# Attention's query projection as seven Strassen products, its sums placed beside the keys' product

## The chip, the cores and the metric

The kernel runs on one core of one Trainium2 chip, in one launch. The metric is the device time of one execution in microseconds (us). The core has five engines with queues of their own: TensorE (PE) for matmuls, VectorE (DVE), ScalarE (ACT), GpSimd (POOL), and SyncE (SP), from whose queue the large transfers are issued. Matmuls read SBUF and write PSUM, and only DVE and ACT take results out of PSUM in this kernel.

## The reference, cut to what matters

One encoder layer is applied to two groups of 256 tokens, so the kernel has 512 rows of 1024 channels. After a layer norm, one wide projection `x @ w_in` gives the inputs of three branches (an mLSTM, a grouped-query attention, a cross-attention into 256 memory tokens). The branches are projected, gated, added and projected once more. A residual layer norm and a gated convolutional feed-forward network follow. The change is in one slice of `x @ w_in`, the attention's queries:

```python
proj = x @ w_in
q_m, k_m, v_m, o_m, g_m, q_a, k_a, v_a, q_c, g_br = split_cols(proj, IN_SPLITS)   # q_a: 1024 columns
qa = apply_axial_rope(rms_norm(q_a.reshape(B, T, ATTN_HEADS, ATTN_DH), attn_q_norm_g), ang_r, ang_c)
ka = apply_axial_rope(rms_norm(k_a.reshape(B, T, KV_HEADS, ATTN_DH), attn_k_norm_g), ang_r, ang_c)
h_a = blocked_attention(qa.reshape(B, T, KV_HEADS, ATTN_GROUP, ATTN_DH), ka, v_a.reshape(B, T, KV_HEADS, ATTN_DH))
```

## The kernel before

**Matmuls.** Every large product is done in three terms. Both operands are split into a high part, rounded to the matmul's type by a cast on ACT, and a low part, the difference, by a subtraction on DVE. The three terms are high x high, high x low and low x high. A weight chunk is 128 x 1024 values: `load_chunk` (L97) loads it into a ring of three tiles "raw", and `split_chunk` (L110, L111) splits it into rings "hi" and "lo" of six tiles each. The transposed input xT has eight k tiles of 128 channels, each a pair of high and low tiles of 128 x 512.

**Jobs.** The program is a list of jobs. `add_nat` makes one for each pair of k tiles (24 matmuls of 512 columns). Its results, one PSUM bank for each of four row tiles, are evacuated in the last job. `run_jobs` (L188) runs the jobs in order and, after each of them, takes steps from the queue `side`, so many that it is empty at the next flush: here one step for each job. In this stretch the jobs are four of the cross-attention's queries ("qc"), one that queues the cross-attention's steps, four of the keys and values ("kv"), four and four of the attention's queries ("qa", "qb"), one that queues the attention's steps, and then the gates and branches ("gc", "bc" and so on).

**Side steps.** The cross-attention has eight units, four heads by two groups, in eleven steps (`attend`). Step i does the values of unit i-2, the transposes of unit i-1 ("pt", L422) and the scores of unit i ("sc"). Scores are followed by maximum (L401), exponentials (L405), reciprocal (L409) and scaling (L411). The transposed probabilities are split into "probTh" and "probTl" (L84, L85). `ev_rope` copies a result out of PSUM into a tile "rx" (L767) and queues a step that normalises and rotates it (L779 to L800). The keys' four such steps stand in `side` behind the cross-attention.

**What sets the order.** Outside a block at the start that is ordered by hand, the tile framework lays down each engine's order before the run. It goes by the order of the program, but lets later instructions pass one whose operands or tile are not there yet. Tiles of one tag share one ring and are handed out in the order in which the program asks for them. Rings that matter here: "a" (62 tiles of 128 x 512: activations, probabilities, "rx"), "hi", "lo" and "raw" for weights, and two in PSUM of four banks each, "pd" for large products and "pa" for scores, transposes and values. On the chip each engine then runs its list strictly in order.

The feed-forward network's down projection (L1120 and on) is already done in Strassen's form over seven pairs of its k tiles, with a transfer that adds in flight on POOL's queue (L1187).

## Time and profile before

| | us |
|---|---|
| median of 3 runs | 943.24 |
| lowest and highest run | 941.63, 943.36 |
| the profiled execution | 943.72 |
| its span (first to last instruction) | 941.9 |
| PE busy | 927.8 |
| DVE busy | 601.2 |
| ACT busy | 408.2 |
| POOL busy | 105.1 |

The span lies 1.8 us below the time of the profiled execution, which is 0.5 us above the median. A matmul of 512 columns is drawn 0.39 us long while the next one starts earlier, so the cost of a matmul has to be read from one start to the next. Weight loads run beside the matmuls.

### The profile page before, as it was taken

Reading aid. Unit: us, or ns where it says so; the run is one execution under the profiler, and the core shown is the slowest. Engines: PE = TensorE matmul, PEld = TensorE weight load, DVE = VectorE, ACT = ScalarE, POOL = GpSimd, SP = SyncE. Lnnn points to the kernel's source line nnn. Section 1 sums busy time; section 2 is a strip of 40 time slices with the busy share of each in tenths; the row PEclk is TensorE's granted clock in tenths of the full one; section 3 lists DMA queues with packets and bytes.
Section 4 is the critical chain, followed back from the end, with each engine's and each line's share of the span. In section 5 each row is a group of like instructions: output and inputs, shape, how many; then the busy total and the mean of one; then the engine's idle time right before and its main releaser. Section 6 shows DMA issues by size and latency. Waiting matters only on the chain. (4 is left out here: it accounts for less than half of the span.)

```text
span 941.9 us, 12380 instructions
## 1 busy us (share of the span) xinstructions
PE 927.8 (99%) x4633; PEld 788.8 (84%) x4633; DVE 601.2 (64%) x1139; ACT 408.2 (43%) x765; POOL 105.1 (11%) x106
## 2 busy tenths in 40 slices
PE   8999999999999999999999999999999999999995
PEld 6888888888889998888888889988888888888885
DVE  4584444896777535366667649655565655666998
ACT  4562543434555435344335312533333333445860
POOL 0100100350000000122007401000000000013301
PEclk9999999999999999999999999999999999999998
DMA  8354223224211243433235432333333333386522
GB/s 291 90 157 144 79 68 90 70 66 120 65 46 44 66 134 90 122 104 111 68 102 189 132 114 68 111 103 99 90 101 100 90 102 100 127 263 133 101 58 89
DMA packets 126671, 101.27 MB, mean 108 GB/s; under 512 B 4240, under 2 KB 106644, under 8 KB 126612
## 3 DMA queue, kind: packets, MB, share of 16 engines
q1 hardware_dynamic: 123588, 94.99, 33.3%
q0 software_dynamic: 3024, 5.51, 3.5%
q8 instruction: 36, 0.59, 0.3%
q14 instruction: 23, 0.19, 0.1%
HBM read 92.86 MB, written 2.11 MB: 101 GB/s over the span
## 5 line engine op out<-in xcount | busy, mean ns | idle before, releaser
L111 DVE TENSOR_TENSOR wlo<-raw,whi 128x1024 fp32r<-128x1024 f32 (+3 forms) x148 | 176.1, 1194 | 213.5 <-ACT whi L110 213.3
L110 ACT CAST whi<-raw 128x1024 fp32r<-128x1024 f32 (+3 forms) x148 | 148.2, 1009 | 298.7 <-PE ua L123 72.0
L1187 POOL DMA_DIRECT2D b<-b x21 | 18.6, 947 | 291.0 <-ACT xop L1227 272.5
L1281 PE MATMUL dn<-wop,xop 128*128 128x512 f32 (+1 forms) x105 | 39.5, 376 | 1.0 <-DVE y L1272 1.0
L1282 PE MATMUL dn<-wop,xop 128*128 128x512 f32 (+1 forms) x105 | 39.4, 375 | 0.0
L1283 PE MATMUL dn<-wop,xop 128*128 128x512 f32 (+1 forms) x105 | 39.3, 375 | 0.0
L1228 DVE TENSOR_TENSOR wop<-b,wop 128x512 fp32r<-128x512 f32 x49 | 33.0, 684 | 6.6 <-ACT wop L1227 6.5
L405 ACT ACTIVATE prob<-sc,nmax 128x256 f32<-128x256 f32 x48 | 22.5, 476 | 24.8 <-DVE nmax L401 24.8
L1227 ACT CAST wop<-b 128x512 fp32r<-128x512 f32 x49 | 29.5, 617 | 7.2 <-PE dn L1283 2.8
L1108 ACT ACTIVATE up<-up 128x512 f32<-128x512 f32 x22 | 13.9, 633 | 42.4 <-DVE up L476 42.4
L115 POOL TENSOR_TENSOR rss<-rss,mhalf 128x4 f32<-128x4 f32 (+1 forms) x12 | 22.6, 1886 | 75.5 <-DVE rss L784 75.5
L1281 PEld LDWEIGHTS dn<-wop,xop 128*128 128x128 f32 x105 | 19.8, 188 | 4.9 <-DVE y L1272 1.3
L1282 PEld LDWEIGHTS dn<-wop,xop 128*128 128x128 f32 x105 | 19.8, 188 | 3.6
L1283 PEld LDWEIGHTS dn<-wop,xop 128*128 128x128 f32 x105 | 19.8, 188 | 3.6
L401 DVE TENSOR_REDUCE nmax<-sc 128x2 f32<-128x512 f32 x24 | 16.4, 682 | 4.3 <-PE sc L124 4.3
L1186 ACT ACTIVATE b<-b 128x512 f32<-128x512 f32 x21 | 13.0, 630 | 11.8 <-DVE b L1190 8.5
L115 POOL TENSOR_TENSOR lnmv<-lnmv,mhalf 128x1 f32<-128x1 f32 x8 | 7.5, 942 | 90.6 <-DVE lnmv L297 90.6
L85 DVE TENSOR_TENSOR probTl<-pt,probTh 128x512 fp32r<-128x512 f32 x24 | 16.4, 683 | 1.4 <-ACT probTh L84 1.4
L473 DVE SCALAR_TENSOR_TENSOR up<-ub,col,up 128x510 f32<-128x510 f32 x20 | 14.9, 743 | 2.7 <-ACT up L470 2.7
L996 DVE SCALAR_TENSOR_TENSOR gate<-gate,ba 128x512 f32<-128x512 f32 x8 | 5.5, 686 | 17.1 <-PE ba L124 9.2
L334 POOL TENSOR_TENSOR y<-y,gain 128x512 f32<-128x512 f32 x8 | 14.1, 1774 | 18.3 <-ACT y L324 18.3
L470 ACT ACTIVATE up<-ub,col 128x512 f32<-128x512 f32 x20 | 15.6, 778 | 1.2 <-PE ub L124 1.2
(1370 smaller groups left out, 2928.3 us busy)
## 6 DMA issues: line engine op xcount, KB each, us to landing
raw<-in_w_in SPq DMA_DIRECT2D x48, 512.0 KB
raw<-in_w_ffn_up SPq DMA_DIRECT2D x44, 512.0 KB
b<-in_w_ffn_down SPq DMA_DIRECT2D x28, 256.0 KB
b<-b POOLq DMA_DIRECT2D x21, 256.0 KB, 3.9
raw<-in_w_mem_kv SPq DMA_DIRECT2D x8, 512.0 KB
raw<-in_w_branch_attn SPq DMA_DIRECT2D x8, 512.0 KB
raw<-in_w_out SPq DMA_DIRECT2D x8, 512.0 KB
raw<-in_w_ffn_down SPq DMA_DIRECT2D x8, 512.0 KB
```

Of the source, the lines that this page charges most:

```text
L85: nc.vector.tensor_tensor(l, src, h.bitcast(F32), op=ALU.subtract)
L110: nc.scalar.copy(hi[:, s], raw[:, s])
L111: nc.vector.tensor_tensor(lo[:, s], raw[:, s], hi[:, s].bitcast(F32), op=ALU.subtract)
L115: self.nc.gpsimd.tensor_tensor(out, in_, self.mhalf.to_broadcast(list(in_.shape)), op=ALU.pow)
L401: nc.vector.tensor_reduce(nm, s3, axis=AX.X, op=ALU.max, negate=True)
L405: nc.scalar.activation(p[:, qt * T : qt * T + T], s3[:, qt, :], AF.Exp, bias=nm[:, qt : qt + 1], accum_out=rs[:, qt : qt + 1],)
L1187: nc.gpsimd.dma_start(dst, src, accum_op=ALU.add)
L1227: nc.scalar.copy(h, src)
L1228: tt(l, src, h.bitcast(F32), op=ALU.subtract)
L1281: mm(out, xh[:, ts], wh[:, c], start=first and i == 0, stop=False, skip_group_check=go_on)
L1282: mm(out, xh[:, ts], wl[:, c], start=False, stop=False, skip_group_check=go_on)
L1283: mm(out, xl[:, ts], wh[:, c], start=False, stop=i == NP - 1, skip_group_check=go_on)
```

## The change

The 512 rows x 1024 channels times 1024 x 1024 weights of the queries are cut in halves: rows by group (256 and 256), columns 512 and 512, and channels by even and odd k tile, four pairs in all. Strassen's seven products replace eight block products.

* `turn_part` keeps the eight unsplit input tiles z ("affine") in `xz`.
* `q_sums(i)` makes four sums of x for pair i (128 x 256 each) and splits them into tiles "qxop". The four calls become jobs of their own, one ahead of each of the keys' four jobs.
* `q_load` loads the weights by k tile: five tiles go into rings "hi" and "lo", three into "raw". The first four loads and the preparation of the first two operands are two more jobs, ahead of the keys' last one. The other four loads are a job behind it.
* `q_prepare` splits a weight operand of 128 x 512 for each product and pair, up to five ahead, and makes the next sum of weights in place: a subtraction on DVE, or a negation on ACT and an adding transfer on POOL's queue (`q_late`).
* `q_product` runs 24 matmuls: four pairs, two row tiles, three terms. Products 1, 6, 7 and 4 gather in one pair of PSUM banks, 5, 3 and 2 in another. `q_copy` and `q_done` copy a partial result out and add the next one to it. `ev_rope` gets an entry `rows` that takes a tile already in SBUF.

So the jobs of this stretch are now: four "qc", the cross-attention's queueing, sums 0, kv 0, sums 1, kv 1, sums 2, kv 2, sums 3, loads, preparation, kv 3, loads, seven products, the attention's queueing.

```diff
--- before.py
+++ after.py
@@ -345,7 +345,7 @@
                 r[h], pair[t // 2][0, (t % 2) * P : (t % 2) * P + P, h * 512 : h * 512 + 512]
             )
 
-    def turn_part(self, rows, ts, out, name, fs=(0, KT), affine=None):
+    def turn_part(self, rows, ts, out, name, fs=(0, KT), affine=None, keep=None):
 
 
         nc = self.nc
@@ -374,6 +374,8 @@
                         bias=affine[1][:, f : f + 1], scale=affine[0][:, f : f + 1],
                     )
                     nc.vector.tensor_copy(hi, z)
+                    if keep is not None:
+                        keep[f] = z
             for j in range(per):
                 hi, lo = [z[:, cs] for z in out[f0 + j]]
                 src = src_of[f0 + j] if affine else ps[:, j * n : j * n + n]
@@ -762,9 +764,12 @@
     def ev_rope(self, parts):
 
         def f(t, ps):
+            x = self.a("rx")
+            self.nc.scalar.copy(x, ps)
+            rows(t, x)
+
+        def rows(t, x):
             nc = self.nc
-            x = self.a("rx")
-            nc.scalar.copy(x, ps)
             for col, nh, which, sink, (mul, add) in parts:
                 n = nh * P
                 xs = x[:, col : col + n]
@@ -803,6 +808,8 @@
                     sink(t, t2)
 
                 self.side.append(step)
+
+        f.rows = rows
         return f
 
 
@@ -907,7 +914,7 @@
             mem.clear()
 
             jobs, self.jobs = self.jobs, []
-            qcT = {}
+            qcT, xz = {}, {}
             self.add_stat(
                 w_in, C_QC, HC, [LazyPair(xT, k) for k in range(KT)], ev_split(qcT, "qcT", SCALE), "qc"
             )
@@ -916,11 +923,12 @@
                     kc[i + 2].get()
                 else:
                     f = (i - 2) * 4
-                    self.turn_part(x, range(NTT), xT, f"xT{i}", (f, f + 4), (lncol[:, 0], lncol[:, 1]))
+                    self.turn_part(x, range(NTT), xT, f"xT{i}", (f, f + 4), (lncol[:, 0], lncol[:, 1]), xz)
                     self.jobs[i - 2][0][0].get()
                 run()
         x.clear()
         xT = [xT[k] for k in range(KT)]
+        mm, tt = nc.tensor.matmul, nc.vector.tensor_tensor
         self.side.append(self.late_constants)
 
 
@@ -961,8 +969,123 @@
             w_in, C_KV, 512, xT,
             self.ev_rope([(0, 2, "k", rows_of("k"), one_k), (256, 2, None, v_sink, one_k)]), "kv",
         )
-        self.add_nat(w_in, C_QA, 512, xT, self.ev_rope([(0, 4, "q", rows_of("q0"), one_q)]), "qa")
-        self.add_nat(w_in, C_QA + 512, 512, xT, self.ev_rope([(0, 4, "q", rows_of("q1"), one_q)]), "qb")
+
+
+        NQ = KT // 2
+        qraw, qx, qops, qmade = {}, {}, {}, []
+        ev_q = [self.ev_rope([(0, 4, "q", rows_of(f"q{n}"), one_q)]).rows for n in range(2)]
+
+        def q_load(i, r):
+
+            k = 2 * i + r
+            pool, tag = (self.wraw, "raw") if r and i else (self.whl, ("hi", "lo")[(i + r) % 2])
+            z = pool.tile([P, 1024], F32, tag=tag, name="qraw")
+            nc.sync.dma_start(z, w_in[k * P : k * P + P, C_QA : C_QA + 1024])
+            for c in range(2):
+                qraw[i, r, c] = z[:, c * 512 : c * 512 + 512]
+
+        def q_sums(i):
+            z, zz = xz.pop(2 * i), xz.pop(2 * i + 1)
+            s12 = self.a("qs")
+            s1, s2 = s12[:, :T], s12[:, T:]
+            s3, s4 = z[:, T:], zz[:, :T]
+            tt(s1, z[:, T:], zz[:, T:], op=ALU.add)
+            tt(s3, z[:, :T], z[:, T:], op=ALU.subtract)
+            tt(s2, s1, z[:, :T], op=ALU.subtract)
+            tt(s4, zz[:, :T], s2, op=ALU.subtract)
+            for p, src in ((5, s1), (6, s2), (3, s4), (7, s3)):
+                o = self.a("qxop", F32R)
+                h, l = o[:, :T], o[:, T:]
+                nc.scalar.copy(h, src)
+                tt(l, src, h.bitcast(F32), op=ALU.subtract)
+                qx[p, i] = (h, l)
+            for p, k, g in ((1, 2 * i, 0), (2, 2 * i + 1, 0), (4, 2 * i + 1, 1)):
+                qx[p, i] = [w[:, g * T : g * T + T] for w in xT[k]]
+
+        QP = {1: (0, 0), 5: (0, 0), 6: (0, 0), 3: (1, 1), 7: (0, 1), 2: (1, 0), 4: (0, 0)}
+        qsteps = [(p, i) for p in QP for i in range(NQ)]
+
+        def q_late(dst, src):
+
+            nc.scalar.activation(dst, dst, AF.Copy, scale=-1.0)
+            nc.gpsimd.dma_start(dst, src, accum_op=ALU.add)
+
+        def q_prepare(n):
+            while len(qmade) < min(n, len(qsteps)):
+                p, i = qsteps[len(qmade)]
+                src = qraw[(i, *QP[p])]
+                w = self.whl.tile([P, 1024], F32R, tag=("hi", "lo")[len(qmade) % 2], name="qwop")
+                h, l = w[:, :512], w[:, 512:]
+                nc.scalar.copy(h, src)
+                tt(l, src, h.bitcast(F32), op=ALU.subtract)
+                qops[p, i] = (h, l)
+                qmade.append((p, i))
+                b = lambda r, c: qraw[i, r, c]
+                if p == 1:
+                    tt(b(0, 0), b(0, 1), b(0, 0), op=ALU.subtract)
+                elif p == 5:
+                    q_late(b(0, 0), b(1, 1))
+                    q_late(b(0, 1), b(1, 1))
+                elif p == 6:
+                    q_late(b(0, 0), b(1, 0))
+                for q, key in ((3, (1, 1)), (7, (0, 1)), (2, (1, 0)), (4, (0, 0))):
+                    if p == q:
+                        del qraw[(i, *key)]
+
+        banks = {}
+
+        def q_product(p, bank, new, done):
+            def run():
+                if new:
+                    banks[bank] = [self.ps(f"q{bank}{j}", dense=True) for j in range(2)]
+                n = list(QP).index(p) * NQ
+                for i in range(NQ):
+                    q_prepare(n + i + 1 + 4)
+                    wh, wl = qops.pop((p, i))
+                    xh, xl = qx.pop((p, i))
+                    for j in range(2):
+                        o, js, skip = banks[bank][j], slice(j * P, j * P + P), not new
+                        mm(o, xh[:, js], wh, start=new and i == 0, stop=False, skip_group_check=skip)
+                        mm(o, xh[:, js], wl, start=False, stop=False, skip_group_check=skip)
+                        mm(o, xl[:, js], wh, start=False, stop=i == NQ - 1, skip_group_check=skip)
+                for j in range(2):
+                    done(j, banks[bank][j])
+            return run
+
+        qacc = {}
+
+        def q_copy(key):
+            def f(j, ps):
+                qacc[key, j] = self.a("rx")
+                nc.scalar.copy(qacc[key, j], ps)
+            return f
+
+        def q_done(key, r, c):
+            def f(j, ps):
+                z = qacc.pop((key, j))
+                tt(z, z, ps, op=ALU.add)
+                ev_q[c](2 * r + j, z)
+            return f
+
+        def q_last(j, ps):
+            z = self.a("rx")
+            nc.scalar.copy(z, ps)
+            ev_q[0](2 + j, z)
+
+
+        n = len(self.jobs) - NQ
+        for i in reversed(range(NQ)):
+            self.jobs.insert(n + i, ([], lambda i=i: q_sums(i)))
+        self.jobs.insert(len(self.jobs) - 1, ([], lambda: [q_load(i, 0) for i in range(NQ)]))
+        self.jobs.insert(len(self.jobs) - 1, ([], lambda: q_prepare(2)))
+        self.add(lambda: [q_load(i, 1) for i in range(NQ)])
+        self.add(q_product(1, "a", True, q_copy("11")))
+        self.add(q_product(5, "b", True, q_copy("22")))
+        self.add(q_product(6, "a", False, q_copy("12")))
+        self.add(q_product(3, "b", False, q_done("12", 0, 1)))
+        self.add(q_product(7, "a", False, q_done("22", 1, 1)))
+        self.add(q_product(2, "b", True, q_done("11", 0, 0)))
+        self.add(q_product(4, "a", False, q_last))
 
         def attention():
             for h in range(2):
@@ -1083,7 +1206,6 @@
 
         PL = NF - 2 * NP
         sums = {}
-        tt = nc.vector.tensor_tensor
 
         def A(i, r, c):
             return hf[PL + 2 * i + c][:, r * T : r * T + T]
@@ -1157,7 +1279,6 @@
         w_dn = io["w_ffn_down"][0]
         acc = {}
         raw, ops = {}, {}
-        mm = nc.tensor.matmul
 
         def down_mm(f, t, half, wh, wl):
             down_split(f)
```

## Rows read from the trace of the kernel before

**Rows 1.** The page's part 1: busy us (share of the span) x instructions.

```profile
PE 927.8 (99%) x4633; PEld 788.8 (84%) x4633; DVE 601.2 (64%) x1139; ACT 408.2 (43%) x765; POOL 105.1 (11%) x106
```

**Rows 2.** Timeline of PE, the keys' first chunk: start us, us, engine, line, op, out<-in.

```profile
83.58 0.39 PE L170 MATMUL kv<-whi,xT20h 128*128 128x512 f32 x1
...
89.02 0.28 PE L122 MATMUL sc<-kcT0h,qcT0h 128*128 128x256 f32 x1
```

**Rows 3.** Timeline of PE, one whole step of the cross-attention between two chunks.

```profile
101.81 0.28 PE L122 MATMUL o<-probTh,vc0h 128*128 128x256 f32 x1
...
102.52 0.60 PE L422 MATMUL pt<-ident,prob 128*128 128x128 f32 x4
102.88 0.36 PE L122 MATMUL sc<-kcT1h,qcT1h 128*128 128x256 f32 x1
...
103.67 0.39 PE L170 MATMUL kv<-whi,xT36h 128*128 128x512 f32 x1
```

**Rows 4.** Busy us by stretch: keys' product; down projection. PE, PEld, DVE, ACT, POOL, PEclk, DMA.

```profile
83.60:111.00 27.40, 27.40 (x145) 23.54 (x144) 10.90 (x20) 12.98 (x28) 2.17 (x3) 1.00 0.32 97
...
860.00:890.00 30.00, 30.00 (x134) 24.85 (x133) 26.25 (x55) 23.64 (x53) 9.48 (x11) 1.00 0.54 97
```

**Rows 5.** Groups of instructions, down projection's splits: busy us, mean ns, idle before.

```profile
L1228 DVE TENSOR_TENSOR wop<-b,wop 128x512 fp32r<-128x512 f32 x49 | 33.0, 684 | 6.6 <-ACT wop L1227 6.5
L1227 ACT CAST wop<-b 128x512 fp32r<-128x512 f32 x49 | 29.5, 617 | 7.2 <-PE dn L1283 2.8 <-PE dn L1169 2.2 <-PE dn L1168 1.3
L1228 DVE TENSOR_TENSOR xop<-hf,xop 128x256 fp32r<-128x256 f32 x28 | 11.7, 416 | 4.1 <-ACT xop L1227 4.0
```

**Rows 6.** Timeline of all engines, one link from transposes to the next transposes.

```profile
242.49 0.30 PE L422 MATMUL pt<-ident,prob 128*128 128x128 f32 x1
...
243.90 0.69 DVE L85 TENSOR_TENSOR probTl<-pt,probTh 128x512 fp32r<-128x512 f32 x1 [1.29 <-ACT probTh L84]
244.50 0.68 DVE L401 TENSOR_REDUCE nmax<-sc 128x2 f32<-128x512 f32 x1
245.22 0.47 ACT L405 ACTIVATE prob<-sc,nmax 128x256 f32<-128x256 f32 x1 [1.35 <-DVE nmax L401]
...
246.27 0.17 DVE L409 RECIPROCAL rsum<-rsum 128x2 f32<-128x2 f32 x1 [1.09 <-ACT prob L405]
...
246.47 0.62 DVE L411 TENSOR_SCALAR prob<-prob,rsum 128x256 f32<-128x256 f32 x2
...
246.67 0.39 PE L122 MATMUL qk<-xT20h,whi 128*128 128x512 f32 x1
...
246.97 0.50 PE L422 MATMUL pt<-ident,prob 128*128 128x128 f32 x2
```

**Rows 7.** Timeline of ACT: a keys' copy, and the keys' first rotary step.

```profile
106.51 0.58 ACT L767 COPY rx<-kv 128x512 f32<-128x512 f32 x1
...
153.59 0.59 ACT L87 ACTIVATE att3h<-o 128x512 fp32r<-128x512 f32 x1
154.08 0.41 ACT L779 ACTIVATE rt<-rx 128x256 f32<-128x256 f32 x1
```

**Rows 8.** Timelines of PE and DVE: two transposes with a chunk's split between them.

```profile
231.84 0.60 PE L422 MATMUL pt<-ident,prob 128*128 128x128 f32 x4
...
232.18 1.23 DVE L111 TENSOR_TENSOR wlo<-raw,whi 128x1024 fp32r<-128x1024 f32 x1 [3.00 <-ACT whi L110]
...
236.89 0.60 PE L422 MATMUL pt<-ident,prob 128*128 128x128 f32 x4
```

**Rows 9.** Timeline of PE near the start: a wait of 2.31 us.

```profile
8.10 0.75 PE L837 MATMUL vc<-whi,mT00h 128*128 128x512 f32 x1 [2.31 <-ACT whi L110]
```

**Rows 10.** PE alone by 1-us stretches: stretch, length, busy (x), PEclk, DMA.

```profile
8.00:9.00 1.00, 0.90 (x2) 0.59 1.05 406
9.00:10.00 1.00, 1.00 (x3) 0.50 1.06 410
...
11.00:12.00 1.00, 1.00 (x8) 0.70 1.07 395
```

## The prediction

> **What bounds the kernel now.** I read the page's busy times first. TensorE (PE) is busy for 927.8 of 941.9 us [rows 1], so the kernel is bound by what PE has to issue. A busy share is not a price, though: matmuls overlap, and each is drawn 0.39 us long. The price is the step from one start to the next. The timeline of the keys' product gives it: its first chunk is 24 matmuls of 512 columns, the first starts at 83.58, and the work behind them starts at 89.02 [rows 2]. That is 5.44 us, or 0.227 us a matmul. Between chunks PE does one step of the cross-attention: values 0.71 us, transposes of the probabilities 0.36 us, next scores 0.79 us [rows 3]. In the whole stretch from 83.6 to 111 PE shows no hole, while VectorE (DVE) works 10.9 and ScalarE (ACT) 13.0 of its 27.4 us [rows 4].
>
> **What is removed.** The query projection is now 2 x 96 = 192 matmuls of 512 columns. Strassen's form is 7 products x 4 pairs x 2 row tiles x 3 terms = 168. So 24 go, and 24 x 0.227 = 5.4 us leave PE. Everything that PE does later is bound by PE too, so this gain would reach the end in full. The Trainium skill (TensorE: Matmul & The Clock Gate, Back-to-back issue gap) gives a smaller pitch for a stream of weight loads and matmuls of 512 columns, about 131 ns. By that the saving would be an estimated 3.1 us; the row shows 227 ns.
>
> **What is added to DVE and ACT.** Weights: 28 splits of 128x512 instead of 8 of 128x1024, each 0.62 us on ACT and 0.68 us on DVE [rows 5]. Sums of x: per pair four additions and four low parts on DVE, eight operations at the 0.42 us of the row of that shape, 3.3 us in all, and four casts on ACT [rows 5]. Further, 12 negations on ACT with 12 accumulating transfers on the POOL queue, four subtractions of weights, and six additions of products. In the products' own stage this fits: the down projection's Strassen stage, which has the same kind of splits, negations and transfers, keeps PE busy 30.00 of 30.00 us while DVE works 26.25 [rows 4]. Per product of 5.4 us the new stage has four splits (2.7 us of DVE), and in three products two additions (1.4 us). The rotary steps that lie beside them have no reader before the attention turns them, so they can slip. I take 0 for that stage, with bounds of 0 and +2 us; a gain there has no mechanism. The queries' loads carry the same bytes as before, at a DMA share of 0.32 [rows 4]. Three of them hold the ring of raw weights until the sixth product, so on SP's queue the gates' first loads stand behind that. They still get about two products (10.9 us) of lead, and I take 0.
>
> **What is moved, and the wait that this makes.** A side step is run after each job, and jobs without matmuls count. The change inserts six such jobs among the keys' four chunks: four sums, one load, one preparation. The cross-attention has eight units (four heads, two groups). Before, its steps were spread over eleven jobs with matmuls. Now step 0 follows the first sums, step 1 the first chunk, step 2 the second sums, and so on: all eight units are asked for before the fourth chunk's evacuation.
>
> The units form a chain. Scores need the PSUM tile handed out after the transposes of the unit before, and those transposes need its softmax. An undisturbed link can be read: transposes at 242.49, low part 243.90, maximum 244.50, exponentials 245.22, scaling 246.47, next transposes 246.97 [rows 6]. That is 4.48 us, whatever PE does meanwhile. PE is not idle in it: a matmul of the next job (qk, 246.67) is let past the waiting transposes [rows 6]. So while keys' matmuls remain they fill the links. When they run out, nothing does. The first product needs PSUM banks of the dense ring, which has four, and the keys hold all four until ACT has copied them to tiles "rx". Tiles of the large ring are handed out in program order: the keys' first rotary step, whose input was copied at 106.51, started only at 154.08, right behind the last cross-attention tile at 153.59 [rows 7]. The keys' copies are now asked for after the eighth unit's probabilities, so they wait for the whole chain.
>
> PE's work up to the first product: 96 x 0.227 = 21.8, eight scores 6.3, eight transposes 2.9, seven values 5.0, together 36.0 us. Without waiting PE would be at the first product at 83.6 + 36.0 = 119.6.
>
> The chain: scores of unit 0 and the first chunk come first (83.6 + 0.8 + 5.4 = 89.8). Then come seven links, then 1.4 us from the last transposes to the start of the low part [rows 6], and one copy of 0.6 us [rows 7] that frees a bank. So the first product starts at 91.8 + 7 links. At 4.48 us that is 123.2, a wait of 3.6 us. With a 128x1024 split in between, a link took 5.05 us (231.84 to 236.89), and the one after it 5.60 us (236.89 to 242.49) [rows 6, 8]. At 5.60 the product starts at 131.0, a wait of 11.4 us. Three links carry a pair's sums. DVE's operations of a clean link take 2.2 us (0.69, 0.68, 0.17, 0.62) [rows 6], which leaves some 2.3 us, and 3.3 us must go in, so I take 5.2 us. The other four get the first weight splits (0.68 us each) in their gaps; between 4.48 and 5.05 I take 4.75. The sum of the seven is 34.6, the product starts at 126.4, and PE waits 6.8 us. The queues behind that wait: on PE the first product and all that follows; on ACT the keys' copies, in order behind the low part of the eighth unit.
>
> **The clock.** The rows hold one place where PE waited in pieces: 2.31 us before 8.10, after small transposes. The granted clock there is at the lower level (1.2 GHz) for parts of four 1-us slices: 0.59, 0.50, 0.50 (alike), 0.70 [rows 9, 10]. At full speed that is 0.41 + 0.50 + 0.50 + 0.30 = 1.7 us lost. The wait here comes in pieces of 2 to 3 us, between 1-us pieces of transposes and scores, for some 9 us. I take one fall, 1.7 us; bounds are 0 (the fall ends before the first product) and two of them, 3.4. The Trainium skill (TensorE: Matmul & The Clock Gate, Loop structure matters more than you think) says that waits between matmul bursts let the array go cold. By that rule the 1.7 us belongs in the sum, and the row agrees; without it the sum below would be +1.4 us.
>
> **Sum.** -5.4 + 6.8 + 1.7 = +3.1 us. The profiled execution took 943.7 us, of which 941.9 is its span [rows 1] and 1.8 lies around it. The median of the runs is 943.2, 0.5 lower. 943.2 + 3.1 = 946.3 us. From here on 0.2% is 1.9 us, about what a measurement of this kernel can tell from no change.
>
> **Rivals.**
> A, the clean chain: all seven links near 4.48 us and no fall of the clock. -5.4 + 3.6 = -1.8 us; with links of 4.9 it is +1.1. So 941.4 to 944.3, point 942.8: no difference. For it: sums of 0.42 us are small pieces that fit into gaps. Against it: only one link that short stands in the rows, and it had no other work on DVE.
> B, faster: the chain does not end last. If the sums are worked off early (DVE has little to do while the cross-attention's own projection runs) and the keys' banks are copied as soon as their matmuls end, the first product's matmuls fill the late links. Then the gain of 5.4 us stays, less some 0 to 2: 937.8 to 940.5, point 938.5. For it: PE lets later matmuls past. Against it: the order in which the large ring hands out tiles [rows 7]. It decides where a keys' copy stands ahead of the last probabilities.
> C, much slower: links of 5.60 us throughout, as with two splits in a row, and a fall. -5.4 + 11.4 + 1.7 = +7.7, 950.9 us. The point from which it decides is a DVE with no free time left in a link. The large ring (62 tiles) would push the same way: the sums hold 20 more tiles and eight are kept from the transposes.
> D, the change does not do what it says: the matmul count stays at 192. The code's loops speak against it; I give it nothing.
>
> **How the numbers follow.** Forecast (chain last, links 4.6 to 5.3, clock falls): 946.3, its own range 944.5 to 949.5, chance 0.46. A: 0.23. B: 0.18. C: 0.13. The range has to leave out no more than 2 in 10: below 939.0 lies about half of B, above 950.5 about half of C, some 0.16 in all. So it goes from 939.0 to 950.5. Faster by over 0.2% (below 941.3) is B, 0.18. Slower (above 945.1) is C and nine tenths of the forecast, 0.54. The rest, 0.28, lies within 0.2%.
>
> **What would show it.** In the profile after, 24 fewer matmuls and a pitch of 0.227 us in the products. Between the first transposes of the cross-attention and the eighth, 33 to 36 us. The keys' copies behind the eighth low part, at about 126 us. PE idle 5 to 9 us between 115 and 127, ended by DVE or ACT, and a granted clock below 1 there. From the first product on, PE without holes. I am wrong if PE is full in that stretch (B), if the waits stand inside the products, where DVE would then be late (the 0 for that stage falls), or if the links are nearer 4.5 or 5.6 us than 4.95.

## The result: 950.4 us, and where the time went

The changed kernel takes 950.36 us (median of 4 runs, 947.88 to 953.10) against 943.1 for the kernel before: a ratio of 1.0086, 95% interval 1.0071 to 1.0100. Slower was the forecast, but by 3.1 us; it is 7.3. A second set of runs gave 950.08 (947.92 to 952.09), 1.0088 (1.0071 to 1.0104).

The page's part 1 of the changed kernel answers to [rows 1]. TensorE (PE) has 24 matmuls less and is yet busy for 3.6 us more; VectorE (DVE) works 27.7 us more.

```profile
span 951.3 us, 12506 instructions
...
PE 931.4 (98%) x4609; PEld 788.2 (83%) x4609; DVE 628.9 (66%) x1201; ACT 428.0 (45%) x813; POOL 120.8 (13%) x118
```

A sum over the whole span doesn't tell where. I cut it at starts of work that both kernels have: the keys' product (kv), the first matmul of the query projection, the end of the last, the gates' stage "ga" behind the attention, the down projection "dn". Busy us by stretch (PE, PEld, DVE, ACT, POOL, then PE's granted clock, DMA share, GB/s), first the kernel before:

```profile
83.58:111.01 27.43, 27.43 (x146) 23.56 (x144) 10.91 (x20) 13.01 (x28) 2.17 (x3) 1.00 0.32 96
111.01:164.22 53.21, 53.21 (x275) 45.54 (x274) 25.25 (x49) 21.92 (x46) 2.29 (x2) 1.00 0.28 80
164.22:356.04 191.82, 191.38 (x1080) 170.71 (x1080) 131.11 (x272) 88.97 (x183) 23.45 (x16) 1.00 0.28 77
...
821.47:941.90 120.43, 110.91 (x508) 92.31 (x506) 95.86 (x189) 61.22 (x128) 22.30 (x25) 0.98 0.52 133
```

The same stretches of the changed kernel, in the execution that took 953.10 us:

```profile
83.50:125.51 42.01, 38.94 (x216) 32.19 (x214) 35.90 (x87) 27.71 (x76) 6.22 (x7) 0.95 0.38 82
125.51:168.63 43.12, 42.24 (x175) 34.33 (x175) 35.08 (x87) 28.89 (x52) 17.84 (x16) 0.93 0.36 80
168.63:362.92 194.29, 192.00 (x1082) 170.58 (x1080) 122.58 (x231) 87.81 (x178) 21.52 (x11) 1.00 0.31 87
362.92:828.37 465.45, 465.22 (x2261) 391.31 (x2260) 288.81 (x495) 181.64 (x299) 48.87 (x40) 1.00 0.35 105
828.37:951.30 122.93, 112.52 (x508) 93.44 (x506) 95.94 (x189) 61.02 (x128) 21.68 (x25) 0.97 0.51 130
```

And in a second profiled execution of the same kernel, which took 947.92 us:

```profile
83.64:125.17 41.53, 37.96 (x215) 31.32 (x213) 35.87 (x87) 27.70 (x76) 6.20 (x7) 1.00 0.38 83
125.17:165.84 40.67, 39.58 (x174) 32.23 (x175) 34.96 (x87) 28.37 (x52) 17.82 (x16) 1.00 0.37 85
165.84:360.00 194.16, 191.98 (x1082) 170.55 (x1080) 122.56 (x231) 87.79 (x178) 21.52 (x11) 1.00 0.30 88
...
825.41:946.00 120.59, 110.88 (x508) 92.31 (x506) 95.84 (x189) 61.04 (x128) 21.66 (x25) 0.99 0.52 132
```

Keys and queries together took 80.64 us before; less the 5.44 us of 24 matmuls they would be 75.2. They take 85.13 and 82.20: losses of 9.9 and 7.0. The stretch up to "ga", in which the queries are turned (transposed by PE) and the attention runs, is 2.3 to 2.5 us longer in both. From "ga" to "dn" nothing changes. The last stretch is 0.2 or 2.5 us longer. The keys start 0.1 us sooner in the first and 0.1 us later in the second; with that the differences make +9.4 and +4.1. The times of the two executions less the 943.72 of the profiled one before are 9.4 and 4.2. The median lies between.

**The first loss is the chain.** Timelines of PE and ScalarE (ACT) of the changed kernel: first, seventh and eighth transposes of the cross-attention, the cast of the last probabilities' high part, the first copy of the keys, the first product. They answer to [rows 6] and [rows 7].

```profile
88.99 0.30 PE L424 MATMUL pt<-ident,prob 128*128 128x128 f32 x1
...
119.30 0.33 PE L424 MATMUL pt<-ident,prob 128*128 128x128 f32 x1 [1.41 <-DVE prob L413]
...
123.29 0.41 PE L424 MATMUL pt<-ident,prob 128*128 128x128 f32 x1
...
124.38 0.59 ACT L84 CAST probTh<-pt 128x512 fp32r<-128x512 f32 x1 [1.92 <-PE pt L424]
124.86 0.59 ACT L768 COPY rx<-kv 128x512 f32<-128x512 f32 x1
...
125.51 0.80 PE L1048 MATMUL qa<-qwop,xT20h 128*128 128x512 f32 x1
```

Seven links take 34.3 us, 4.90 each (forecast 34.6). The keys' copy stands right behind the last probabilities, though the last of the keys' matmuls ended at 116.93, and frees the bank for the first product: 42.0 us behind the keys' start, where 36.0 would be dense. The loss is 6.0 us (5.5 in the second execution). PE is drawn idle for only 3.1 us of that stretch (42.01 less 38.94 busy; 3.6 in the second): the rest is work drawn longer than where the matmuls stand close.

**The second is the clock, in one of the two.** PE alone by 1-us stretches (busy, granted clock, DMA share, GB/s), to be read beside [rows 10]:

```profile
120.00:121.00 1.00, 0.80 (x7) 0.99 0.00 0
121.00:122.00 1.00, 0.38 (x1) 0.50 0.72 123
...
130.00:131.00 1.00, 1.00 (x3) 0.50 0.00 0
131.00:132.00 1.00, 1.00 (x5) 0.89 0.00 0
```

From 121.0 to 131.1 PE runs at its lower level (1.2 GHz): 5.1 us by the slices' sum, some 2.7 of them under the first thirteen matmuls of the products (0.427 instead of 0.227 us apart). In the second execution PE waits as long ahead of that place (1.40 and 0.20 us; 1.41 and 0.20 in the first), and each slice there shows 1.00.

**The third is DVE beside the last product**, which I had priced at nothing. Timelines of DVE, whose splits (L1020) answer to those of [rows 5], and of the two matmuls of PE that wait for it:

```profile
159.61 1.22 DVE L111 TENSOR_TENSOR wlo<-raw,whi 128x1024 fp32r<-128x1024 f32 x1
160.75 0.68 DVE L803 TENSOR_TENSOR rt<-rt,rt 128x512 f32<-128x512 f32 x1
161.35 0.68 DVE L1020 TENSOR_TENSOR qwop<-qraw,qwop 128x512 fp32r<-128x512 f32 x1
162.94 0.88 DVE L805 TENSOR_SCALAR rt<-rt,rss 128x128 f32<-128x128 f32 x4 [0.90 <-POOL rss L115]
163.73 1.89 DVE L1020 TENSOR_TENSOR qwop<-qraw,qwop 128x512 fp32r<-128x512 f32 x3
...
162.09 0.50 PE L1049 MATMUL qa<-qwop,xT21h 128*128 128x512 f32 x1 [0.16 <-DVE qwop L1020]
...
164.47 0.49 PE L1049 MATMUL qa<-qwop,xT23h 128*128 128x512 f32 x1 [0.72 <-DVE qwop L1020]
```

The product's weight splits (qwop) stand in DVE's order behind a split for the gates and behind rotary steps; one of these (rt) waits 0.90 us for POOL's square root, with three splits queued behind it. PE's matmuls start 0.55 and 1.12 us apart there instead of 0.227: 1.2 us lost (1.4 in the second execution).

**The fourth is the turning of the queries**, also priced at nothing. Timelines of PE: the one wait of that stage in the kernel before (first line), and those in the changed kernel:

```profile
220.74 0.39 PE L124 MATMUL sc<-kT0h,qTl 128*128 128x256 f32 x1 [0.45 <-DVE qTl L85]
...
195.47 0.33 PE L957 MATMUL rTq<-ident,rt 128*128 128x128 f32 x1 [1.06 <-DVE rt L805]
...
206.43 0.50 PE L424 MATMUL pt<-ident,prob 128*128 128x128 f32 x2 [1.23 <-DVE prob L413]
```

### The profile page after: what moved, and what is told of

Read it like the earlier page. It is cut to its first block, busy times and chain, and to the rows that moved or that the text cites. A ratio compares the mean times of both kernels' runs of the same rounds, so it can differ in the third digit from the quotient of the medians.

```text
span 951.3 us, 12506 instructions
## 1 busy us (share of the span) xinstructions
PE 931.4 (98%) x4609; PEld 788.2 (83%) x4609; DVE 628.9 (66%) x1201; ACT 428.0 (45%) x813; POOL 120.8 (13%) x118
## 5 line engine op out<-in xcount | busy, mean ns | idle before, releaser
L111 DVE TENSOR_TENSOR wlo<-raw,whi 128x1024 fp32r<-128x1024 f32 (+3 forms) x140 | 167.5, 1200 | 190.3 <-ACT whi L110 188.3
L110 ACT CAST whi<-raw 128x1024 fp32r<-128x1024 f32 (+3 forms) x140 | 139.8, 1006 | 262.1 <-PE ua L123 72.0
L1402 PE MATMUL dn<-wop,xop 128*128 128x512 f32 (+1 forms) x105 | 40.2, 383 | 1.9 <-DVE y L1393 1.9
L115 POOL TENSOR_TENSOR rss<-rss,mhalf 128x4 f32<-128x4 f32 (+1 forms) x12 | 30.6, 2550 | 24.9 <-DVE rss L789 24.9
L1020 DVE TENSOR_TENSOR qwop<-qraw,qwop 128x512 fp32r<-128x512 f32 x28 | 18.6, 685 | 6.5 <-ACT qwop L1019 6.5
L1019 ACT CAST qwop<-qraw 128x512 fp32r<-128x512 f32 x28 | 16.8, 619 | 9.8 <-PE qb L1050 3.8
L1011 POOL DMA_DIRECT2D qraw<-qraw x12 | 10.5, 903 | 76.6 <-ACT qraw L1010 69.8
L424 PE MATMUL pt<-ident,prob 128*128 128x128 f32 x96 | 16.3, 283 | 2.6 <-DVE prob L413 2.6
```

Of the source, the lines that this page charges most:

```text
L110: nc.scalar.copy(hi[:, s], raw[:, s])
L111: nc.vector.tensor_tensor(lo[:, s], raw[:, s], hi[:, s].bitcast(F32), op=ALU.subtract)
L115: self.nc.gpsimd.tensor_tensor(out, in_, self.mhalf.to_broadcast(list(in_.shape)), op=ALU.pow)
L1019: nc.scalar.copy(h, src)
L1020: tt(l, src, h.bitcast(F32), op=ALU.subtract)
L1402: mm(out, xh[:, ts], wh[:, c], start=first and i == 0, stop=False, skip_group_check=go_on)
```

## The experiments

The theory (T): the six jobs without matmuls among the keys' chunks press the cross-attention together, its chain ends last, and the keys' copies, handed out in order behind it, hold the first product up. The rival (R): DVE simply has too much to do, 100.5 of 116.5 us between 83.5 and 200 us. The table has, for each kernel, the median, the ratio to the kernel before (run beside it each time, medians of 942.0 to 943.1) with its interval, and from its profile, in us: from the keys' start to the first matmul of the queries, the query projection, from there to "ga", the last stage, and what the granted clock's 1-us slices lost between 84 and 240 us.

| kernel | median | ratio (95%) | to the first | queries | to "ga" | last | clock |
|---|---|---|---|---|---|---|---|
| before | 943.1 | 1 | 27.43 | 53.21 | 191.82 | 120.43 | 0 |
| changed | 950.36 | 1.0086 (1.0071, 1.0100) | 42.01 | 43.12 | 194.29 | 122.93 | 5.1 |
| r_after | 950.08 | 1.0088 (1.0071, 1.0104) | 41.53 | 40.67 | 194.15 | 120.59 | 0 |
| e1_merged | 942.93 | 1.0006 (0.9995, 1.0016) | 27.43 | 47.77 | 195.60 | 121.44 | 1.7 |
| e2_before_empty | 951.74 | 1.0093 (1.0078, 1.0108) | 42.28 | 47.09 | 191.43 | 120.45 | 5.1 |
| e3_no_sums | 947.07 | 1.0050 (1.0035, 1.0065) | 40.07 | 42.15 | 194.11 | 120.77 | 1.7 |
| e4_own_ring | 955.39 | 1.0142 (1.0119, 1.0165) | 33.39 | 50.06 | 194.10 | 124.46 | 1.7 |
| e5_three | 940.33 | 0.9974 (0.9964, 0.9983) | 27.43 | 47.83 | 192.53 | 122.90 | 0 |
| e5_six | 943.29 | 1.0011 (1.0001, 1.0022) | 27.42 | 48.00 | 197.25 | 121.03 | 0 |
| e7_fill | 951.29 | 1.0096 (1.0082, 1.0109) | 43.52 | 42.02 | 193.97 | 120.42 | 0 |
| e8_two | 942.87 | 1.0002 (0.9992, 1.0011) | 35.61 | 44.67 | 191.16 | 123.23 | 1.7 |
| e9_four | 946.56 | 1.0037 (1.0024, 1.0050) | 35.65 | 43.28 | 195.19 | 121.29 | 1.7 |
| e10_before_three | 943.23 | 1.0011 (1.0002, 1.0020) | 27.42 | 53.21 | 191.93 | 120.50 | 0 |
| e11_ring_no_late | 952.12 | 1.0094 (1.0077, 1.0112) | 33.33 | 47.29 | 194.10 | 122.20 | 0 |

**The same work without jobs of its own.** "ahead" runs functions at the head of the job with that index.

```diff
-        for i in reversed(range(NQ)):
-            self.jobs.insert(n + i, ([], lambda i=i: q_sums(i)))
-        self.jobs.insert(len(self.jobs) - 1, ([], lambda: [q_load(i, 0) for i in range(NQ)]))
-        self.jobs.insert(len(self.jobs) - 1, ([], lambda: q_prepare(2)))
-        self.add(lambda: [q_load(i, 1) for i in range(NQ)])
+        for i in range(NQ - 1):
+            ahead(n + i, lambda i=i: q_sums(i))
+        ahead(
+            n + NQ - 1, lambda: q_sums(NQ - 1),
+            lambda: [q_load(i, 0) for i in range(NQ)], lambda: q_prepare(2),
+        )
         self.add(q_product(1, "a", True, q_copy("11")))
+        ahead(len(self.jobs) - 1, lambda: [q_load(i, 1) for i in range(NQ)])
```

> The changed kernel with the six jobs that have no matmuls (sums, loads, preparation) run at the head of the keys' four chunks, and the seventh at the head of the first product: the same instructions, but one step of the cross-attention per job with matmuls again. Theory T (the six jobs press the cross-attention's chain together, it ends last, and the keys' copies wait behind it): no wait before the first product, no clock fall there; the 6.0 us and 2.7 us that the changed kernel lost there come back: 950.4 - 8.7 = 941.7 us, up to 945 if the softmax work that now lies beside the products makes their weight splits later. Rival R (VectorE simply has too much to do between 83 and 200 us, 100 of 116 us, wherever the steps lie): the waits move into the products and the turning of the queries, 949 to 951 us.

942.93: 7.4 us came back, and T's range holds. The first product starts 27.43 us behind the keys' start, as before, and the query projection is 5.44 us shorter: the 24 matmuls, to the hundredth. That all of DVE's work stayed and the waits in the products went speaks against R. Yet the time is only that of the kernel before: 3.8 us are lost up to "ga". ACT and PE there:

```profile
217.62 1.04 ACT L110 CAST whi<-raw 128x1024 fp32r<-128x1024 f32 x1 [3.27 <-DMA raw<-in_w_in]
218.57 0.59 ACT L1116 ACTIVATE gate<-gc 128x512 f32<-128x512 f32 x1
219.06 0.58 ACT L84 CAST qTh<-rTq 128x512 fp32r<-128x512 f32 x1
...
219.69 0.54 PE L122 MATMUL sc<-kT0h,qTh 128*128 128x256 f32 x1 [2.45 <-ACT qTh L84]
```

The raw tile for that cast could be loaded only when DVE had split the one before it, and DVE had rotary steps ahead of that split; the queries' cast is queued behind the waiting cast. PE waits 2.45 us, and the clock falls once (1.7 us). DVE's share of busy time doesn't tell why it was late: 38.99 of 45.50 us from 158.5 to 204 here, 35.01 of 39.78 us from 164.22 to 204 in the kernel before.

**The jobs alone.**

```diff
+        n = len(self.jobs) - 4
+        for i in reversed(range(4)):
+            self.jobs.insert(n + i, ([], lambda: None))
+        for _ in range(2):
+            self.jobs.insert(len(self.jobs) - 1, ([], lambda: None))
```

> The kernel before, with six jobs that do nothing put between the keys' chunks at the places where the change puts its own: no instruction is added, only the cross-attention's steps are asked for sooner. T: the chain ends last here too, with links of 4.5 to 4.9 us; PE waits 3.5 to 6 us before the queries' first matmul and the clock may fall once (0 to 2.7 us): 946.6 to 951.8, point 948.5. R: VectorE has nothing more to do, so 943.1 and no wait.

951.74: six jobs that do nothing cost the kernel before 8.9 us, at the upper end of T's range and far from R. The first and eighth transposes, the last cast, the keys' copy and the first query matmul:

```profile
89.12 0.27 PE L422 MATMUL pt<-ident,prob 128*128 128x128 f32 x1
...
123.68 0.45 PE L422 MATMUL pt<-ident,prob 128*128 128x128 f32 x1 [1.12 <-DVE prob L411]
...
124.81 0.58 ACT L84 CAST probTh<-pt 128x512 fp32r<-128x512 f32 x1 [1.86 <-PE pt L422]
125.29 0.59 ACT L767 COPY rx<-kv 128x512 f32<-128x512 f32 x1
...
125.93 0.80 PE L170 MATMUL qa<-whi,xT20h 128*128 128x512 f32 x1
```

The chain takes 34.56 us (89.12 to 123.68), 4.94 a link, without any of the change's work on DVE: here the keys' 128x1024 splits stand between. So a link is not long because of the sums, as I had written: any work that DVE has between does it. The stretch to "ga" is not longer (191.43). Empty jobs also bring weights later, as `run_jobs` asks for them up to three jobs ahead, but no matmul up to "ga" waits for a weight's split here: all of PE's waits are for the cross-attention's probabilities (3.4 us).

**The jobs without the sums.**

```diff
         def q_sums(i):
-            z, zz = xz.pop(2 * i), xz.pop(2 * i + 1)
...
+            for p in (5, 6, 3, 7):
+                qx[p, i] = [w[:, :T] for w in xT[2 * i]]
```

> The changed kernel without the sums of x: products 5, 6, 3 and 7 take the unchanged halves of x instead (so their values are not the projection's), the 32 operations on VectorE and 16 casts on ScalarE beside the keys' product are left out, the jobs stay. T: the chain still ends last, with links of 4.5 to 4.7 us instead of 4.9; the first product starts about 2 us earlier than in the changed kernel (123.5 instead of 125.5) and the clock falls all the same: 947 to 949 us. R: without 13 us of VectorE's work the waits go, the 24 matmuls are gained in full: 937.7 to 940 us.

947.07, in T's range. Seven links take 32.7 us (87.59 to 120.31), and the first product comes 1.9 us earlier. The waits in the last product (0.27 and 0.72 us) and at the turning (1.05 and 1.11) are all there: the sums don't cause them.

**The keys' banks freed early.**

```diff
-NA = 62
+NA = 58
-            x = self.a("rx")
+            x = self.acts.tile([P, 512], F32, tag="rxk", name="rxk", bufs=4)
```

> The changed kernel with the keys' four copies in a ring of four tiles of their own (the large ring has 58 instead of 62), so that they needn't be handed out after the last probabilities; everything else, the seven extra jobs too, as in the changed kernel. T: the keys' banks come free as soon as their matmuls end, the first product's matmuls fill the last links of the chain; first product before 118 us, no clock fall: 950.4 - 8.7 = 941.7, bounds 940 and 944. If the order of the large ring is not what holds the banks: first product at 125 as before, 949 to 951.

The mechanism came out, the time did not: the first product starts 8.6 us sooner (33.39), so it is the ring's order that held the banks, but the kernel takes 955.39. What is late next is a transfer. ACT and PE, first a keys' copy, now ahead of the last probabilities, and the first product:

```profile
112.31 0.59 ACT L768 COPY rxk<-kv 128x512 f32<-128x512 f32 x1 [0.18 <-PE kv L172]
...
116.87 0.40 PE L1048 MATMUL qa<-qwop,xT20h 128*128 128x512 f32 x1
...
126.67 0.62 ACT L1019 CAST qwop<-qraw 128x512 fp32r<-128x512 f32 x1 [2.88 <-DMA qraw<-qraw]
127.19 0.62 ACT L1010 ACTIVATE qraw<-qraw 128x512 f32<-128x512 f32 x1
127.72 0.56 ACT L84 CAST probTh<-pt 128x512 fp32r<-128x512 f32 x1
...
128.34 0.58 PE L122 MATMUL o<-probTh,vc2h 128*128 128x256 f32 x1 [2.22 <-ACT probTh L84]
```

The sixth product's first weights wait for their accumulating transfer, the last unit's probabilities are queued behind that cast, PE waits 2.22 us for them and the clock falls (1.7). A further 2.44 and 0.71 us pass in the last product, where PE waits for DVE, and between "ga" and "dn" it takes 3.2 us more (468.61 for 465.43; 468.20 in the next kernel, 465.4 in all with 62 tiles), which is the price of the smaller ring and so of the experiment. The next kernel takes the transfers away, with the negations; its products are then not the projection's.

```diff
                 elif p == 5:
-                    q_late(b(0, 0), b(1, 1))
-                    q_late(b(0, 1), b(1, 1))
-                elif p == 6:
-                    q_late(b(0, 0), b(1, 0))
+                    pass
```

> The kernel e4_own_ring without the 12 negations and 12 accumulating transfers: the blocks of weights stay as they are after the first subtraction, so the products' values are not the projection's. In e4_own_ring ScalarE waited 2.88 us for such a transfer at 126.7, with the last unit's probabilities queued behind it, PE waited 2.2 us for those, and the clock fell (1.7 us). Theory (with the banks free early, the transfers come last): wait and fall go, 955.4 - 3.9 = 951.5, bounds 950 and 953; the rest of its excess, from the ring of 58 tiles (3.2 us between 361 and 830 us) and from the last product's splits (3.4 us at 158 to 163), stays. Rival (the wait there is the chain's own, whatever ScalarE does): 955.

952.12: wait and fall are gone, 3.3 us less, in the range. The accumulating transfers (with their negations), which cost nothing while the chain held the products up, do cost where they start early. What stays is DVE: in the last product PE waits 4.1 us for it, where the changed kernel waits 0.9:

```profile
159.38 0.50 PE L1046 MATMUL qa<-qwop,xT21h 128*128 128x512 f32 x1 [3.33 <-DVE qwop L1020]
```

So keys and queries together still take 80.62 us, 5.4 above the 75.2 and only 1.6 below the changed kernel's second execution. With the banks free, most of the time that the chain had cost is lost in waiting for DVE instead. That is R's part in it; that DVE's sum of work alone decides is ruled out by e1_merged, where PE waits nowhere in the products.

**Where the steps lie.** To e1_merged, three or six jobs that do nothing are added behind products, where the keys' banks are long free:

```diff
         self.add(q_product(7, "a", False, q_done("22", 1, 1)))
+        self.add(lambda: None)
         self.add(q_product(2, "b", True, q_done("11", 0, 0)))
+        self.add(lambda: None)
         self.add(q_product(4, "a", False, q_last))
+        self.add(lambda: None)
```

> The kernel e1_merged with three jobs that do nothing, one behind each of the products 7, 2 and 4: there all eight units of the cross-attention have been asked for (its last transposes stood at 146.4 us in e1_merged), so that three of the rotary steps come about 16 us sooner. In e1_merged VectorE had 10 us free beside the products (37.6 of 47.6) and almost none behind them, and PE's one large wait (2.45 us at 219.7, then a low clock for 1.9 us) came of that backlog. Theory (what is left of the loss is the place of the rotary steps on VectorE): that wait and its clock fall go, 942.9 - 3.9 = 939.0, bounds 938 and 941. Rival (VectorE's sum of work decides, or the attention that is asked for three jobs sooner waits in the same way): 942 to 944.

940.33, 0.26% faster than the kernel before (0.17 to 0.36%): the wait at 219.7 and its fall of the clock are gone, and up to "ga" 0.7 us are lost instead of 3.8. From the keys' start to "dn" it takes 733.2 us for 737.9: of the 5.4 us, 4.7 are kept. In the median 2.6 remain; its profile has 2.5 more in the last stage.

```diff
         self.add(q_product(6, "a", False, q_copy("12")))
+        self.add(lambda: None)
         self.add(q_product(3, "b", False, q_done("12", 0, 1)))
+        self.add(lambda: None)
...
         self.add(q_product(4, "a", False, q_last))
+        self.add(lambda: None)
+        self.add(lambda: None)
```

> The kernel e1_merged with six jobs that do nothing behind the products 6, 3, 7, 2 and 4 (two behind the last): as many extra steps as in the changed kernel, but none of them among the keys' chunks. If jobs without matmuls cost by their place (among the keys, ahead of the copies that free the banks): no wait before the first product; rotary steps lie between the weight splits of the last products as in the changed kernel, which had 1.2 us of waits there and 1.9 us more at the turning of the queries: 939 to 942.5. If they cost wherever they lie, as each presses two steps into one job: 945 to 950.

943.29, 0.8 above the first range and 1.7 below the second. There is no wait ahead of the first product and none in the products, so an extra step costs by its place. But three more rotary steps stand among the gates' first splits: PE waits three times there for DVE's wlo, 4.2 us in all. Waits of PE between 83 and 360 us (sum, times, longest):

```profile
PE gc L124 <- DVE wlo L111: 4.2, 3, 1.6
```

A control tells whether the steps alone would have gained that:

```diff
+        for _ in range(2):
+            self.jobs.insert(len(self.jobs) - 1, ([], lambda: None))
+        self.add(lambda: None)
```

> The kernel before with three jobs that do nothing, two ahead of the last chunk of the query projection and one behind it: the same three extra steps at the same place as in e5_three, but without Strassen's products. It tells whether e5_three's 2.6 us come of the 24 matmuls or of the steps' place. Theory (the matmuls): the kernel before has one wait of 0.44 us in its middle, at 220.7, so there is nothing more to win: 942.5 to 943.3. Rival (the steps' place): 940.3.

943.23, 0.1% slower than the kernel before beside it (0.02 to 0.20%); from the keys' start to "dn" it is the same to 0.1 us (737.9). So the steps' place alone gains nothing; e5_three's gain needs the 24 matmuls to be gone.

**How many jobs the keys bear.** Sums at the head of the chunks, load and preparation as jobs (e8_two), and the other way round (e9_four).

```diff
-        for i in reversed(range(NQ)):
-            self.jobs.insert(n + i, ([], lambda i=i: q_sums(i)))
+        for i in range(NQ):
+            ahead(n + i, lambda i=i: q_sums(i))
         self.jobs.insert(len(self.jobs) - 1, ([], lambda: [q_load(i, 0) for i in range(NQ)]))
         self.jobs.insert(len(self.jobs) - 1, ([], lambda: q_prepare(2)))
```

> The changed kernel with the four sums run at the head of the keys' chunks (no job of their own) and the load and the preparation left as two jobs ahead of the fourth chunk. Now four instead of eight units of the cross-attention are asked for ahead of the keys' copies (two in e1_merged). Theory as a point from which it decides: the fourth unit's transposes come at about 112 us, no later than PE's dense arrival at the first product (83.5 + 21.8 + five scores 4.0 + four transposes 1.4 + four values 2.8 = 113.5), so there is no wait: the first product starts by 114.5 and the time is that of e1_merged or, with the rotary steps three jobs earlier, of e5_three: 940 to 943. Rival (each extra job among the keys costs its sixth of the 8.7 us): 943 + 2.9 = 945.8.

```diff
+        ahead(n + NQ - 1, lambda: [q_load(i, 0) for i in range(NQ)], lambda: q_prepare(2))
         for i in reversed(range(NQ)):
             self.jobs.insert(n + i, ([], lambda i=i: q_sums(i)))
-        self.jobs.insert(len(self.jobs) - 1, ([], lambda: [q_load(i, 0) for i in range(NQ)]))
-        self.jobs.insert(len(self.jobs) - 1, ([], lambda: q_prepare(2)))
```

> The changed kernel with load and preparation run at the head of the keys' fourth chunk, and the four sums left as jobs of their own: six units of the cross-attention are asked for ahead of the keys' copies. Theory: the sixth unit's transposes come at 89.0 + 5 x 4.9 = 113.5, a bank is free at 115.5; PE's dense arrival is 83.5 + 21.8 + 7 x 0.79 + 6 x 0.36 + 5 x 0.71 = 116.5: hardly a wait (0 to 1 us), no fall of the clock from it; then the waits in the products and at the turning as in the changed kernel (3 us): 943 to 945.5. Rival (a sixth of 8.7 us a job): 943 + 5.8 = 948.8.

942.87 with two and 946.56 with four, where a sixth of the price for each job would be 945.8 and 948.8: the rival fails in both. But so does my account of e8_two. Its first product starts 35.61 us behind the keys' start, where I had allowed 31.0 at the latest. PE and ACT there, the fifth unit's transposes, the casts of the sums, the first copy of the keys and the first product:

```profile
117.24 0.47 PE L424 MATMUL pt<-ident,prob 128*128 128x128 f32 x1 [1.90 <-DVE prob L413]
...
117.94 0.71 ACT L999 CAST qxop<-affine 128x256 fp32r<-128x256 f32 x2 [0.57 <-DVE affine L995]
118.56 0.58 ACT L768 COPY rx<-kv 128x512 f32<-128x512 f32 x1
...
119.44 0.63 PE L1048 MATMUL qa<-qwop,xT20h 128*128 128x512 f32 x1
```

PE waits 1.90 us for the fifth unit, the clock falls once (1.7), and the copy stands behind casts that wait for DVE's sums. Keys and queries together take 80.28 us, 5.1 above the 75.2; in e9_four, where PE waits 1.27 us for the keys' copy at 118.20, they take 78.93, 3.7 above it. What e8_two loses there it has back up to "ga", where it takes 191.16 us for e1_merged's 195.60; e9_four, with a wait of 3.1 us at the turning, takes 195.19. So the equal medians of e8_two and e1_merged don't mean that two jobs are free: a price and a gain cancel. A number of jobs from which they begin to cost isn't shown.

**The clock.** Small matmuls, 12 each ahead of the transposes of the last two units, fill the waits ahead of the fall:

```diff
             pt = self.ps(f"pt{h}{g}")
+            for _ in range(fill.get((h, g), 0)):
+                nc.tensor.matmul(pt[:, :P], self.ident, self.ident, start=True, stop=True)
...
+                    {(3, 0): 12, (3, 1): 12},
```

> The changed kernel with 12 small matmuls (128 columns, 0.11 us each at 5.3 us of its trace) ahead of the transposes of the seventh and of the eighth unit of the cross-attention, into the tile that the transposes then overwrite: they fill waits of PE at 118 to 123 us and change nothing else. Theory (the clock falls at 121.0 because of these waits, and costs some 0.4 us before the first product and 2.7 us behind it): no fall, granted clock 1.00 through 131 us, the products' stage 2.7 us shorter, 950.4 - 3 = 947.4, bounds 946.5 and 948.5. Rival (the fall has another cause, or it comes a few us later at the waits that stay): 950 to 951.5.

951.29. This profile has no fall (granted clock 1.00 from 84 to 240 us), but the time is no shorter. Each of these matmuls has two records in the trace, 0.11 us from start to start:

```profile
122.24 2.17 PE L423 MATMUL pt<-ident 128*128 128x128 f32 x18
```

So 12 take 2.6 us and not 1.3, and they made the links longer: the last transposes stand at 124.25 for 123.29, and the first product starts 1.5 us later. In the last product PE waits 2.9 us for DVE instead of 0.9. So this kernel doesn't measure the clock's price, and as the repeat has no fall either, it isn't shown that the filling kept the clock up:

> The changed kernel again, for a second profile of it. Behind the keys' product everything up to the start of the down projection should again come 6.9 to 7.0 us later than in the kernel before. The first profile lost 2.4 us more in the last stage (waits of 0.9 and 1.0 us more at 927 to 934 us and a clock fall), though the instructions of that stage are the same in the same order: if that is the execution's own, the second profile has a last stage of 120.4 to 121.5 us instead of 122.9; if it belongs to the change, 122.9 again. Median 950.4, bounds 949.5 and 951.5.

Its profiled execution has no fall, and keys and queries together are 2.9 us shorter (82.20 for 85.13). The eight runs of the changed kernel stand in the order of their mean clocks: 0.998 and 0.996 at 947.9, 0.994 at 949.6 to 950.2, 0.993 and 0.992 at 951.1 and 952.1, 0.989 at 953.1 (means of whole executions, with the last stage's falls). So the fall is not a fixed cost of the change but something its waits lay it open to. That everything up to "dn" would come 6.9 us later again, as I expected, was wrong: 3.9. The last stage was the execution's own, 120.59.

## Why the forecast was right in kind and too small

- **24 matmuls, 5.4 us**: right. 5.44 in e1_merged, where nothing lay on top.
- **Dilution, chain, copies behind it**: right, and shown from both sides (e1_merged takes it away, e2_before_empty makes it without the change). First product forecast at 126.4, seen at 125.5 and 125.2; links 4.90 for 4.95; wait 6.0 and 5.5 for 6.8. The mean link came out with some luck. Single links run from 3.99 to 6.25 us, and the sums, which I took for the main cause, lengthen a link by only 0.23 us on average (4.90 against 4.67 in e3_no_sums). The 5.2 us of a link with sums is also less than the 5.5 that its own 2.2 and 3.3 us on DVE make. Two signs that I had named failed: PE is drawn idle for 3.1 and 3.6 us there, not 5 to 9, and the keys' copies stand behind the cast of the high part (124.38), not behind the low part, which DVE starts at 125.00, after the first copy.
- **The clock, 1.7 with bounds 0 and 3.4**: mis-sized. It cost 0 in one execution and about 3 in the other (2.7 behind the first product, the rest in its later start). The fall of the first execution was 5.1 us by its slices, longer than the one I had taken for a model (1.7). The place was right; one price for it is not to be had. The Trainium skill (TensorE: Matmul & The Clock Gate, Loop structure matters more than you think) says that a long wait for a transfer between matmuls makes PE go cold. Here the waits are short (1.41 us the longest) and are ended by DVE or ACT, and the same ones led to a fall in one execution and not in the other: these traces show a risk and no price.
- **"I take 0 for that stage"**: this step failed. The products lost 1.2 to 1.4 us, within the bounds I had given but not at the value I took. The down projection, from which I took it, has no rotary steps; here they stand in DVE's order ahead of the last product's splits, and one waits for POOL.
- **"They can slip"**: this failed too, and cost most, 2.3 to 2.5 us up to "ga", outside any bound that I had given. The rotary steps' reader is the turning, and the same extra jobs that I charged with the chain also bring the attention sooner: its first scores start 32.5 us behind the last query matmul, 55.7 us in the kernel before. e2_before_empty has them at 31.2 us without the products' work and loses nothing (191.43); e3_no_sums has jobs and products without the sums and loses 2.3 (194.11). So early demand costs only together with DVE's work for the products. It costs in e9_four and e5_six as well (39.4 and 40.2 us; 3.4 and 5.4 lost). Late demand costs with it too: e1_merged, at 61.0 us, loses 3.8 by another wait. Between them, at 47.5 us, e5_three loses 0.7 and e8_two nothing. Which single step's place makes the price isn't isolated further.

The two terms that I had put at nothing measured 3.7 us together in both executions (1.2 + 2.5, 1.4 + 2.3), most of the 4.2 us by which the median lies above the forecast. The chain and the clock, forecast at 8.5, measured 8.7 and 5.5.

With the measured terms the sum is -5.4 + 5.5 + 1.4 + 2.3 = +3.8 for the second execution and -5.4 + 6.0 + 2.7 + 1.2 + 2.5 = +7.0 for the first; the rest of their +4.2 and +9.4 is the last stage (0.2 and 2.5) and the start. Rival C gave a like time (950.9) by links of 5.60 us throughout, where the mean was 4.90. The median stands at the range's upper end (950.5), outside the forecast's own range (to 949.5).

**Open**: the last stage. It has the same instructions in the same order in all these kernels but the two with 58 tiles (e4_own_ring, e11_ring_no_late), where DVE's and ACT's orders differ. It took 120.4 to 120.5 us in the three profiles without Strassen's query products, and 120.4 to 124.5 in the eleven with them, in two of which it was 120.4 and 120.6. In the long ones PE waits up to 2.8 us for the sum "y", DVE for a product, and a fall of the clock can follow. What makes these executions differ isn't shown.

## What to carry to other kernels

Where a list of jobs also paces other work, a job has a price even if it does nothing: count what it makes come sooner, and what that holds when it comes. Put work without matmuls into jobs that have some. A share of busy time doesn't say whether an engine can hide more: DVE is 88% busy in the down projection's stage, from which I took the 0, and 81 to 86% beside the products, where PE waited for it. For each piece said to slip, name its first reader and add up the engine's work until then, in the order in which it stands. A saving survives only if that order is right: the same 24 matmuls made +7.3, 0 and -2.6 us.

## What the runs showed of the hardware

The same program with waits of the same length fell to the lower clock for some 10 us in one execution (5.1 us by its slices) and not at all in another. Between 84 and 240 us a profile had no fall, one of 1.7 us (five kernels) or one of 5.1 us (the changed kernel and e2_before_empty). A wait's length doesn't tell: falls of 1.7 us came with waits of 2.45 us in e1_merged and 2.22 us in e4_own_ring, while waits of 3.14 us in e9_four, 3.33 us in e11_ring_no_late and 2.17 us in e7_fill had none behind them. A 128x128 matmul of f32 data leaves two records that start 0.11 us apart (e7_fill), where a transposition of the same size leaves one.
